# A layout of steps by a planner: small products ahead of all dense ones on TensorE

## The chip, the cores and the metric

The kernel runs on one core of a Trainium2 chip. The core has five engines with a queue each: TensorE (PE; its weight loads are listed as PEld), VectorE (DVE), ScalarE (ACT), GpSimd (POOL) and SyncE (SP, which here only issues DMAs). Each engine takes its instructions strictly in the order of its own queue, so an instruction that waits holds up all that stand behind it there. The metric is the device time of one execution in microseconds. Before the change the median of three runs is 2429.49 us (2426.96 to 2431.29).

## The reference

One decoder layer on 2048 tokens of width 1024, with 256 memory tokens. Three branches read one projection of the normed input; each branch's output is gated, projected, weighted by sigmoid gates, summed, projected once more and added to the input.

```
h = rms_norm(x, norm_g)
p = h @ w_in                      # 1024 -> 7552 columns, split into
                                  # r, k, v, decay, a, z_a | q, k, v, z_b | xq, z_c | gates
y_a = rwkv7_mix(r, k, v, decay, a, ...) * silu(z_a)      # 8 heads x 64, delta rule over time
y_b = sliding_window_sink_attn(q, k, v, ...) * silu(z_b) # 8 heads, 2 kv heads, window 128
y_c = memory_cross_attn(xq, mem, ...) * silu(z_c)        # 4 heads x 128
merged = sum_i sigmoid(gate_i) * (y_i @ w_proj_i)
out = x + merged @ w_out
```

The recurrence of branch A, per head and token, on a 64 x 64 state S:

```
sa = S @ a_t
S  = S * w_t + sa b_t^T + v_t k_t^T
y  = S @ r_t
```

## The kernel before

The 2048 tokens are worked in four superblocks of 512. Within a superblock two streams are written out and woven together by estimated durations (`weave`): `stream_r` with branch A, and `stream_f` with branches C and B, the merges of their outputs and the gates. Then follow the merge of branch A, the norm of the next superblock's input (`x_norm`) and the output projection.

**Dense and small products.** The large projections are done at about float32 accuracy as three products of fp32r halves (`gemm3`, L411 to L418: high x high, high x low, low x high). The planner calls every product whose moving operand is fp32r *dense*; its tile is 128 x 128. All others, in plain float32, are here called *small*: the transposes through TensorE (L450, L477, L724, L745, L830, L906, L1016), the column sums for norms (L466), the decay products (L637, L639), the chunk products of branch A (L694, L734, L751, L780 to L801) and the attention's products with V (L910, L1021). Many of them use only a part of the array: 64 x 64 or 32 x 32.

**Branch A's pair of heads.** `rwkv_prep` prepares a pair of heads for eight chunks of 64 tokens. VectorE builds QE, QO and BK (to L684); TensorE multiplies them in four groups of four, eight records each (L694); VectorE masks the results (L696, L697) into AB and QE, QO; ScalarE copies the diagonal blocks (L703); VectorE inverts the small triangles in 31 steps of three operations (L710 to L712); ScalarE writes the inverse into AB (L718); TensorE applies it (L734, L751), with a copy by VectorE (L735) between the two halves. V is projected, shifted (L607 to L610), transposed (L745) and copied into Z. Then `rwkv_chain` runs the chunks one after another: L787, L790 (VectorE), L795, L798 and L799 (VectorE), L801, L802 (VectorE).

**Tiles.** PSUM holds two tiles each for `mm` (projections), `rw` (branch A) and `as_` (attention), and one each for `oo` and `yps`. The tiles of one tag are opened in the order of the program, and one is free again when its last user is done.

**The planner.** The order on each engine is not the program's. `steps` reads all instructions of the program, with what each must come after, and gives each a rank: its place in the program, less 1000 for the loads and splits of weights, less 600 for what reads PSUM on other engines, and 500 more for the triangle inversion on VectorE. `lay_out` then plays the program through with a clock for each engine and estimated costs. In each turn it takes the engine that can begin soonest, lists the steps that are ready on it by then (`can`, L220) and picks one. For all engines but PE that is the step of the lowest rank. For PE it is the same, unless the tile last used was not 128 x 128: then steps of that same tile come first, and after them the lowest rank (L223, L224). A change of tile costs 95 ns in its clock, and a dense product after a small one 95 ns more. `order` puts the resulting sequences into the program, so what the planner picks is the order in which the chip's queues hold the instructions.

Of the kernel before, what the change touches and what calls it, by code (L numbers as in the profile page):

```python
# [158 lines left out]
def lay_out(tc, todo):  # L159

    metas = {tag: meta.bufs for p in tc.info.pools if p.space != bass.MemoryType.DRAM for tag, meta in p.tag_meta.items()}
    source = {t.name: t.source_name for t in tc.info.tiles}
    tags = {tag: Tag(b) for tag, b in metas.items()}
    users, opened = {}, set()
    for s in todo:
        for name in {r[0] for r in s.reads + s.writes}:
            users.setdefault(name, []).append(s)
        for r in s.writes:
            if source[r[0]] in tags and r[0] not in opened:
                opened.add(r[0])  # L170
                s.opens.append(r[0])
                tags[source[r[0]]].queue.append(r[0])
    left = {name: len(u) for name, u in users.items()}
    heads = {tag: 0 for tag in tags}
    clock = {e: 0.0 for e in NAMES.values()}
    ready, parked = {e: {} for e in clock}, set()
    orders = {e: [] for e in clock}
    missing = {s: len(s.before) for s in todo}

    def seen_by(s, b):  # L180

        if b.eng == s.eng:
            return 0 if s.eng == "PE" else b.end + 30
        return b.end + LAT[s.eng]

    def room(s):

        at = 0.0
        for name in s.opens:
            t = tags[source[name]]  # L190
            if t.queue[heads[source[name]]] != name or not t.free:
                return None
            old = t.free[0]
            if old:
                at = max([at] + [seen_by(s, b) for b in last[old].values()])
        return at

    def offer(s):
        at = room(s)
        if at is None:  # L200
            parked.add(s)
            ready[s.eng].pop(s, None)
        else:
            parked.discard(s)
            ready[s.eng][s] = max([at] + [seen_by(s, b) for b in s.before])

    last = {name: {} for name in users}
    for s in todo:
        if not missing[s]:
            offer(s)  # L210
    tile, fp32, wires = (128, 128), False, 0
    for _ in todo:
        best = None
        for e, rs in ready.items():
            if rs:
                at = max(clock[e], min(rs.values()))
                if best is None or at < best[0]:
                    best = at, e
        at, e = best
        can = [s for s, t in ready[e].items() if t <= at]  # L220
        s = min(can, key=lambda s: s.rank)
        if e == "PE":
            if tile != (128, 128) and s.tile != tile:  # L223
                s = min(can, key=lambda s: (s.tile != tile, s.rank))  # L224
            if s.tile != tile:
                at += 95
            clock[e] = at + s.busy
            if s.dense and fp32:
                clock[e] += 95
            elif s.tile != tile and s.tile[1] < 128:  # L230
                clock[e] += 49
            tile, fp32 = s.tile, not s.dense
        else:
            clock[e] = at + s.busy
        s.end = at + s.dur
        if s.bytes:
            wires = s.end = max(wires, s.end) + s.bytes / 330
        del ready[e][s]
        orders[e].append(s)
        again = set()  # L240
        for name in s.opens:
            tag = source[name]
            tags[tag].free.pop(0)
            heads[tag] += 1
            again.add(tag)
        for name in {r[0] for r in s.reads + s.writes}:
            if e not in last[name] or last[name][e].end < s.end:
                last[name][e] = s
            left[name] -= 1
            if not left[name] and source[name] in tags:  # L250
                tags[source[name]].free.append(name)
                again.add(source[name])
        for a in s.after:
            missing[a] -= 1
            if not missing[a]:
                offer(a)
        if again:
            for a in [a for rs in (parked, *ready.values()) for a in rs if any(source[n] in again for n in a.opens)]:
                offer(a)
    return orders  # L260


def order(tc, manual):

    orders = lay_out(tc, steps(list(tc.nc.cur_bb.bb.instructions), manual))
    how = mybir.DependencyInfo(mybir.DependencyClass.NoSync, mybir.DependencyReason.DATA)
    for l in orders.values():
        for a, b in zip(l, l[1:]):
            tc.add_manual_dep(b.ins, a.ins.name, how, reason="order")
# [952 lines left out]
```

## Time and profile before

| what | value |
|---|---|
| median of the runs | 2429.49 us (2426.96 to 2431.29) |
| the profiled execution | 2420.68 us, span 2418.8 us |
| mean granted TensorE clock over the span | 0.994 |
| TensorE busy | 2371.3 us, 98%, 14496 matmul records |
| VectorE busy | 1550.0 us, 64% |
| ScalarE busy | 884.2 us, 37% |
| GpSimd busy | 120.1 us, 5% |

The profile is of one execution. Times in its rows are microseconds from the start of the span. A row of the timeline has the start, the duration, the engine, the line of the kernel, the operation, the tile that is written and the tiles that are read, the part of the array for matmuls, the shapes, how many like instructions are merged, and in brackets the idle time of the engine just ahead of it with what ended it. A row of the waits has the waiting engine and line, who released it, the total in microseconds, how often and the longest. A row of the stretches has the length and then, for PE, PEld, DVE, ACT and POOL, busy microseconds and the count, then the granted clock (1.00 is full speed), the share of the DMA engines and GB/s. A plain float32 product that is no transpose stands as two records. Matmuls are pipelined, and the end of one is modelled, so that starts tell more than durations.

### The profile page before, as it was taken

Reading aid. Unit: us, or ns where it says so; the run is one execution under the profiler, and the core shown is the slowest. Engines: PE = TensorE matmul, PEld = TensorE weight load, DVE = VectorE, ACT = ScalarE, POOL = GpSimd, SP = SyncE. Lnnn points to the kernel's source line nnn. Section 1 sums busy time; section 2 is a strip of 40 time slices with the busy share of each in tenths; the row PEclk is TensorE's granted clock in tenths of the full one; section 3 lists DMA queues with packets and bytes.
Section 4 is the critical chain, followed back from the end, with each engine's and each line's share of the span. In section 5 each row is a group of like instructions: output and inputs, shape, how many; then the busy total and the mean of one; then the engine's idle time right before and its main releaser. Section 6 shows DMA issues by size and latency. Waiting matters only on the chain.

```text
span 2418.8 us, 39467 instructions
## 1 busy us (share of the span) xinstructions
PE 2371.3 (98%) x14496; PEld 1857.1 (77%) x14496; DVE 1550.0 (64%) x4926; ACT 884.2 (37%) x1961; POOL 120.1 (5%) x175
## 2 busy tenths in 40 slices
PE   7998999999999999999999999999999999999999
PEld 6777777786887777878887777777888777877887
DVE  6878778685567778852238868674143895876312
ACT  5444555434333444332113434443122344334110
POOL 1001000000000010000000001000000001000000
PEclk9998999999998999999999999999999999999999
DMA  6754555576853443446673433435566344243655
GB/s 219 253 189 149 199 195 203 201 254 216 294 180 105 150 141 105 141 141 217 200 251 111 130 116 125 139 117 204 194 209 207 103 146 136 94 140 114 209 191 191
DMA packets 142209, 416.03 MB, mean 172 GB/s; under 512 B 16193, under 2 KB 22721, under 8 KB 142017
## 3 DMA queue, kind: packets, MB, share of 16 engines
q1 hardware_dynamic: 129344, 390.44, 48.1%
q10 hardware_dynamic: 12672, 23.07, 2.8%
q8 instruction: 115, 1.88, 0.3%
q14 instruction: 78, 0.63, 0.1%
HBM read 320.66 MB, written 92.80 MB: 171 GB/s over the span
## 4 chain that ended last, share of the span: by engine, by line
PE 83%; DVE 9%; ACT 3%; DMA 3%; issue 1%; POOL 0%; SPq 0%; ACTq 0%; DVEq 0%
PE mm L416 19%; PE mm L418 19%; PE mm L417 19%; PE rw L694 2%; DMA whl<-in_w_in 2%; PE oo L1021 1%; PE mm L1067 1%; PE mm L1066 1%; PE mm L1065 1%; PE rw L801 1%; PE rw L787 1%; PE oo L910 1%; PE rw L795 1%; PE rw L734 1%; DVE whl L399 1%
## 5 line engine op out<-in xcount | busy, mean ns | idle before, releaser
L416 PE MATMUL mm<-hH,whl 128*128 128x512 f32 x1888 | 759.7, 402 | 4.8 <-ACT g L1032 3.2
L417 PE MATMUL mm<-hL,whl 128*128 128x512 f32 x1888 | 753.2, 399 | 0.0
L418 PE MATMUL mm<-hH,whl 128*128 128x512 f32 x1888 | 753.0, 399 | 0.0
L416 PEld LDWEIGHTS mm<-hH,whl 128*128 128x128 f32 x1888 | 355.4, 188 | 84.7 <-issue 7.7
L418 PEld LDWEIGHTS mm<-hH,whl 128*128 128x128 f32 x1888 | 355.2, 188 | 77.9 <-issue 3.7
L417 PEld LDWEIGHTS mm<-hL,whl 128*128 128x128 f32 x1888 | 355.5, 188 | 69.6 <-issue 1.4
L1047 DVE SCALAR_TENSOR_TENSOR g<-g,mm 128x512 f32<-128x512 f32 x64 | 43.8, 684 | 227.4 <-PE mm L418 227.4
L398 ACT ACTIVATE whl<-whl 128x512 fp32r<-128x512 f32 x174 | 109.3, 629 | 146.7 <-DMA whl<-in_w_in 72.7
L1032 ACT ACTIVATE g<-mm 128x512 f32<-128x512 f32 x96 | 57.1, 595 | 275.4 <-PE mm L418 275.0
L399 DVE TENSOR_TENSOR whl<-whl 128x512 fp32r<-128x512 f32 x174 | 119.6, 687 | 59.5 <-ACT whl L398 57.2
L417 PE MATMUL mm<-yl,whl 128*128 128x512 f32 x384 | 151.0, 393 | 0.0
L416 PE MATMUL mm<-yh,whl 128*128 128x512 f32 x384 | 150.8, 393 | 0.0
L418 PE MATMUL mm<-yh,whl 128*128 128x512 f32 x384 | 150.6, 392 | 0.0
L711 DVE TENSOR_TENSOR ibc<-ibc,Yi 128x248 f32<-128x248 f32 (+30 forms) x496 | 143.9, 290 | 10.1
L710 DVE STREAM_SHUFFLE ibc<-Nc 128x248 f32<-128x248 f32 (+30 forms) x496 | 148.8, 312 | 0.0
L793 ACT ACTIVATE SP<-Z,Pl 64x64 f32<-64x64 f32 x256 | 88.4, 345 | 155.1 <-DVE Z L802 151.5
L712 DVE TENSOR_TENSOR Yi<-Yi,ibc 128x248 f32<-128x248 f32 (+30 forms) x496 | 141.0, 284 | 2.0
L1001 ACT ACTIVATE g<-g,mxs,st 128x256 f32<-128x256 f32 (+1 forms) x128 | 74.4, 585 | 74.8 <-DVE mxs L994 74.8
L802 DVE SCALAR_TENSOR_TENSOR Z<-rw,Pl,SP 64x64 f32<-64x64 f32 x224 | 63.5, 283 | 44.9 <-PE rw L801 41.7
L416 PEld LDWEIGHTS mm<-yh,whl 128*128 128x128 f32 x384 | 72.1, 188 | 15.3 <-DVE g L1047 0.2
L417 PEld LDWEIGHTS mm<-yl,whl 128*128 128x128 f32 x384 | 72.1, 188 | 15.0
L418 PEld LDWEIGHTS mm<-yh,whl 128*128 128x128 f32 x384 | 72.1, 188 | 14.9
(1769 smaller groups left out, 3760.7 us busy)
## 6 DMA issues: line engine op xcount, KB each, us to landing
whl<-k SPq DMA_DIRECT2D x474, 512.0 KB, 3.3
k<-whl SPq DMA_DIRECT2D x158, 512.0 KB, 3.3
whl<-in_w_in SPq DMA_DIRECT2D x118, 256.0 KB, 3.2
g<-in_x ACTq DMA_DIRECT2D x32, 256.0 KB, 5.6
out<-g ACTq DMA_DIRECT2D x32, 256.0 KB, 4.9
whl<-in_w_proj SPq DMA_DIRECT2D x24, 256.0 KB, 2.9
rt<-in_x ACTq DMA_DIRECT2D x24, 256.0 KB, 5.2
km<-mk SPq DMA_DIRECT2D x16, 256.0 KB, 2.7
```

The costliest lines, as they stand in the source:

```text
L398: S.activation(w[:, 0], raw, AF.Copy)
L399: V.tensor_tensor(w[:, 1], raw, w[:, 0].bitcast(F32), op=ALU.subtract)
L416: PE.matmul(out, lh, rh, start=i == 0, stop=False)
L417: PE.matmul(out, lh, rl, start=False, stop=False)
L418: PE.matmul(out, ll, rh, start=False, stop=i == n - 1)
L710: V.stream_shuffle(bc[:, :, :n], Nc[:, :, s + 1:], [s] * 32)
L711: V.tensor_tensor(bc[:, :, :n], bc[:, :, :n], Y[:, :, s:s + 1].to_broadcast([128, NC_, n]), op=ALU.mult)
L712: V.tensor_tensor(Y[:, :, s + 1:], Y[:, :, s + 1:], bc[:, :, :n], op=ALU.add)
L793: S.activation(SP[h, i], Z[h, i, e, c], AF.Copy, scale=g[4][h, c:c + 1])
L802: upds = [V.scalar_tensor_tensor(Sst[h, g[0]] if c == NC_ - 1 else Z[h, i, e, c + 1], pS[h, i], g[4][h, c:c + 1], SP[h, i], op0=ALU.mult, ...
L1001: S.activation(prs[b][:, i, m0:], prs[b][:, i, m0:], AF.Exp, scale=r2[:, b, i:i + 1], bias=mx[:, b, i:i + 1], accum_out=mx[:, b, 2 + i:3 + i])
L1032: S.activation(t, gp, AF.Tanh, scale=0.5)
```

## The change

In `lay_out`, the choice on PE. Before, the lowest rank was taken, or after a tile other than 128 x 128 the same tile first. Now dense steps come after all others that are ready; among the others, those of the tile last used come first if the last product was a small one; within that the lowest rank decides. Nothing else in the planner, in its costs or in the program is different.

```diff
@@ -220,8 +220,7 @@
         can = [s for s, t in ready[e].items() if t <= at]
         s = min(can, key=lambda s: s.rank)
         if e == "PE":
-            if tile != (128, 128) and s.tile != tile:
-                s = min(can, key=lambda s: (s.tile != tile, s.rank))
+            s = min(can, key=lambda s: (s.dense, fp32 and s.tile != tile, s.rank))
             if s.tile != tile:
                 at += 95
             clock[e] = at + s.busy
```

`fp32` is true if the product picked last on PE was a small one. Since the planner's clocks go on from each choice, the sequences of the other engines are drawn anew as well.

## The prediction

> **What bounds the kernel now.** I read the page's busy times first, then PE's own waits, then the timeline round its longest repeated wait, and last the clock by stretches. The page:
>
> ```profile
> span 2418.8 us, 39467 instructions
> PE 2371.3 (98%) x14496; PEld 1857.1 (77%) x14496; DVE 1550.0 (64%) x4926; ACT 884.2 (37%) x1961; POOL 120.1 (5%) x175
> ```
>
> TensorE is busy for 98% of the span. No product is removed or added by the change, so only three things can move the time: PE's idle time (2418.8 - 2371.3 = 47.5 us), the price of switching between dense and small products, and the granted clock. PE's own waits, longest first:
>
> ```profile
> PE rw L450 <- DVE g L445: 10.0, 2, 9.5
> PE rw L734 <- ACT AB L718: 5.6, 3, 1.9
> PE rw L694 <- DVE QE L684: 3.5, 4, 2.6
> ```
>
> The first is the start of the kernel: nothing is there to do before the first loads and the norm, and the change can't touch it. The second is three equal stalls of 1.86 us, one in each of the later three superblocks, ahead of L734 (the products with the inverse of the small triangle). Here they are, two of them with the dense product behind the small stretch that follows:
>
> ```profile
> 739.07 0.66 PE L734 MATMUL rw<-ibc,AB 32*32 32x32 f32 x16 [1.86 <-ACT AB L718]
> 753.44 0.40 PE L416 MATMUL mm<-hH,whl 128*128 128x512 f32 x1
> ...
> 1327.17 0.66 PE L734 MATMUL rw<-ibc,AB 32*32 32x32 f32 x16 [1.86 <-ACT AB L718]
> 1336.34 0.40 PE L416 MATMUL mm<-hH,whl 128*128 128x512 f32 x1
> ...
> 1910.46 0.66 PE L734 MATMUL rw<-ibc,AB 32*32 32x32 f32 x16 [1.85 <-ACT AB L718]
> ```
>
> The reader should see that the projections (L416 to L418) are used up by then, and that the next one into a new `mm` tile comes only after the small products: 9.17 us after L734 in the second superblock drawn here (1336.34 - 1327.17), 14.37 us in the first (753.44 - 739.07). The same work took 5.2 us longer the first time, and the clock says why:
>
> ```profile
> core 0: us, PE busy (x) PEld busy (x) DVE busy (x) ACT busy (x) POOL busy (x), PEclk, DMA share, GB/s
> 694.90:700.00 5.10, 5.10 (x25) 3.95 (x23) 0.56 (x1) 0.00 (x0) 0.10 (x1) 1.00 0.09 26
> 700.00:739.00 39.00, 37.16 (x205) 30.30 (x204) 36.04 (x154) 12.01 (x27) 1.61 (x5) 1.00 0.35 109
> 739.70:753.40 13.70, 13.70 (x83) 9.34 (x83) 3.53 (x9) 5.54 (x16) 1.26 (x2) 0.50 0.03 9
> 1327.20:1340.90 13.70, 13.35 (x119) 10.18 (x120) 5.74 (x13) 9.04 (x25) 1.26 (x2) 1.00 0.16 50
> 1910.40:1924.10 13.70, 13.30 (x118) 10.19 (x119) 5.75 (x13) 9.02 (x26) 1.26 (x2) 1.00 0.11 33
> ```
>
> After the first stall PE ran at half clock for 13.7 us; after the two others at full clock.
>
> **The change, part by part.** *Small ahead of dense.* What a small product gains is the time it now lies ready behind dense ones of lower rank. The stall shows the case that matters. VectorE writes QE and QO, which L694 multiplies:
>
> ```profile
> 694.05 0.69 DVE L684 TENSOR_TENSOR QO<-rr__7309,Pt 64x512 f32<-64x512 f32 x1
> 694.77 0.69 DVE L685 TENSOR_TENSOR rr__7309<-rr__7309,rk__7144 128x512 f32<-128x512 f32 x1
> 700.71 0.69 DVE L848 SCALAR_TENSOR_TENSOR g<-g,mm 128x512 f32<-128x512 f32 x1 [5.25 <-ACT g L847]
> 701.31 0.68 DVE L696 TENSOR_TENSOR AB<-rw,gmask 64x512 f32<-64x512 f32 x1
> ...
> 708.45 0.44 DVE L710 STREAM_SHUFFLE ibc<-Nc 128x248 f32<-128x248 f32 x1
> ...
> 737.28 0.17 DVE L712 TENSOR_TENSOR Yi<-Yi,ibc 128x8 f32<-128x8 f32 x1
> ```
>
> ```profile
> 693.36 1.89 PE L910 MATMUL oo<-g,vm 128*128 128x256 f32 x8
> 694.90 0.58 PE L416 MATMUL mm<-hH,whl 128*128 128x512 f32 x1
> ...
> 699.65 0.39 PE L418 MATMUL mm<-hH,whl 128*128 128x512 f32 x1
> 699.97 0.37 PE L694 MATMUL rw<-QE,BK 64*128 64x128 f32 x1
> ...
> 700.86 0.27 PE L694 MATMUL rw<-QO,BK 64*128 64x128 f32 x1
> 701.07 0.50 PE L416 MATMUL mm<-hH,whl 128*128 128x512 f32 x1
> 701.40 0.39 PE L417 MATMUL mm<-hL,whl 128*128 128x512 f32 x1
> ```
>
> QO is done at 694.74 (694.05 + 0.69). L694 starts at 699.97, 5.2 us later, behind 21 dense products from 694.90 on, and VectorE meanwhile idles 5.25 us. Then it is full: 36.04 of the 39 us from 700 to 739, with the inversion (L710 to L712) from 708.45 to 737.45, whose end PE waits for. With the new choice L694 follows L910 at about 694.9, so the masks (L696, L697) fill VectorE's idle 5.25 us and the inversion can end up to that much earlier, of which PE needs 1.86. The dense products moved back are then still there for PE's gaps around L734. The other two superblocks have the same pattern:
>
> ```profile
> 1282.19 0.69 DVE L684 TENSOR_TENSOR QO<-rr__12827,Pt 64x512 f32<-64x512 f32 x1
> 1288.85 0.69 DVE L848 SCALAR_TENSOR_TENSOR g<-g,mm 128x512 f32<-128x512 f32 x1 [5.25 <-ACT g L847]
> ...
> 1865.51 0.69 DVE L684 TENSOR_TENSOR QO<-rr__18345,Pt 64x512 f32<-64x512 f32 x1
> 1872.17 0.69 DVE L848 SCALAR_TENSOR_TENSOR g<-g,mm 128x512 f32<-128x512 f32 x1 [5.25 <-ACT g L847]
> ```
>
> Bounds of this term: nothing, if the inversion is held by something else, and all three stalls, 3 x 1.86 = 5.6 us. I take -5.6, since 5.25 us of room against 1.86 is ample. What is late next are the hops of the same chain through L735, L745 and L751; the dense products kept back cover them.
>
> *The clock after the stall.* The half clock cost 5.2 us (14.37 - 9.17) behind one stall of three. Bounds: 0 (it comes anyway) and -5.2. I take -5.2: with the idle time gone, nothing in these rows is left that would start the drop.
>
> The Trainium skill (TensorE: Matmul & The Clock Gate, Part 1) says that the clock is gated by activity over free-running windows of about 3.4 us, so that the drop depends on where in a window the idle time falls. That agrees with one drop after three equal stalls; by it the unprofiled runs may hold more or fewer such drops than this profile, which only widens the range.
>
> *More and smaller pieces.* A group taken as soon as it is ready may come in more pieces than a group taken when its rank comes up. The price of a cut:
>
> ```profile
> 968.23 0.40 PE L418 MATMUL mm<-hH,whl 128*128 128x512 f32 x1
> 968.46 0.40 PE L416 MATMUL mm<-hH,whl 128*128 128x512 f32 x1
> 968.70 0.27 PE L477 MATMUL rw<-c_ident,rep 128*128 128x128 f32 x1
> 968.73 0.49 PE L417 MATMUL mm<-hL,whl 128*128 128x512 f32 x1
> 969.05 0.27 PE L477 MATMUL rw<-c_ident,rep 128*128 128x128 f32 x1
> 969.08 0.48 PE L418 MATMUL mm<-hH,whl 128*128 128x512 f32 x1
> ```
>
> Dense starts lie 0.23 apart, and 0.35 with one transpose between (969.08 - 968.73): at least 0.12 with the transpose itself. Round L694 it is 0.09 going in (699.97 - 699.65 - 0.23), 0.10 from the last small start (701.07 - 700.86 - 0.11) and 0.10 at the next dense one (701.40 - 701.07 - 0.23), 0.29 in all. I take 0.2 a cut. How many come or go, the trace doesn't say. L694 above joins the L910 in front of it, which saves one. The rwkv_prep of each of 16 head pairs has four such groups that may split once (+16), and the 16 pairs of branch B, with transposes and products (L1016, L1021) in pieces, may have two more cuts each (+32). Joins like that one there may be one for each of the 12 head pairs of the later superblocks. Bounds: -12 joins and +48 cuts, -2.4 to +9.6 us. I take +10 cuts, +2.0, near the lower end: groups like L734 and L477 in the rows above already follow another engine step by step and go when they are ready, whatever the rule.
>
> *Small ones of the last tile first.* Before, this held after every tile but 128x128; now after every small product. It reorders neighbours inside a run of small products; a switch there costs no more than a cut, either way, at a few places: 0, inside the bounds of the cuts.
>
> *What else moves.* The statistics (L466), the transposes of BK (L724) and of x for the next superblock (L450) and the decay products (L637, L639) also go earlier where they wait behind dense ones. They take their PSUM tiles sooner, but each tag is opened in program order, so that nothing else could have used them. I cost them at nothing: what hides them is the dense supply, and without it they would be on PE's path as they are now. Their readers on ScalarE, VectorE and POOL come earlier, too, and POOL has room (5% busy). No DMA is added; SP's queue with the weights is laid out by the same clock and shifts with it.
>
> *Sum.* Against the profiled execution, 2420.7 us with 2418.8 of span: -5.6 - 5.2 + 2.0 = -8.8, so 2411.9. The median of the runs, 2429.5, lies 8.8 above that execution; the same difference off it gives 2420.7. I round to 2421.
>
> **The rivals.** *A: nothing comes of it.* The whole order is drawn anew, the inversion starts earlier but gets a later place among VectorE's other work (it is the lowest in rank there), and the stall stays. For it: VectorE is 92% busy from 700 to 739 (36.04 of 39). Against: the idle 5.25 us lies ahead of just that stretch. Only the cuts remain: 2429.5 + 2.0 = 2431.5.
>
> *B: the pieces, slower.* If every group splits as above, 48 cuts at 0.2 are 9.6 us; with the clock drop staying they outweigh the stalls from 28 cuts on (5.6 / 0.2). If the stalls stay too, it is 2429.5 + 9.6 = 2439. For it: VectorE releases its transposes' inputs one by one, as L477 shows. Against: the groups of the chain, the most numerous, are already taken when ready.
>
> *C: the clock, slower.* Small products run together leave stretches without dense ones, and each superblock gets a half clock. The stalls go, one drop stays, two come: 2429.5 - 5.6 + 2.0 + 2 x 5.2 = 2436. Against: 1327.20 to 1340.90 was such a stretch, at 1.00.
>
> The Trainium skill (same page, Part 4) says that transposes don't count as activity for the clock as other products do, which speaks for C; no run here shows that yet.
>
> **How the numbers follow.** Forecast 0.58, A 0.17, B 0.18, C 0.07. Differences under 0.2% (4.9 us) can't be told from none. Faster: the forecast with its own range, from 2406 (all three stalls gone, a further two drops of 5.2 gone in runs that have them, joins of 2.4: 2429.5 - 5.6 - 15.6 - 2.4 = 2405.9) to 2424.6: 0.60, with a little of B. Within: A and small sums, 0.14. Slower: B, C and part of A, 0.26. The range that leaves two in ten out reaches from 2405 to 2437.
>
> **What would show it.** Right: L694 starts within 0.5 us of its QO in the first pair of each later superblock; VectorE's wait of 5.25 before L848 is gone; PE's wait for AB L718 falls from 5.6 us to under 1; no half clock near 740; PE's busy time grows by no more than 2 us. Wrong: the wait for L718 is still there; new waits of PE on VectorE of over 1 us (L694, L450, L1021), with dense products queued behind; a half clock in more stretches; PE's busy time up by 5 us or more, which would be the pieces.

## The result and the profile after

The changed kernel takes 2435.81 us (median of ten, 2431.45 to 2441.48) against 2428.68 us for the kernel before (ten runs, 2423.96 to 2433.67): a ratio of 1.0031, with a 95% interval of 1.002 to 1.0042. It is slower by 7 us; 2421 had been forecast, and a gain. The profiled execution took 2435.84 us, with a span of 2434.0. Line numbers after L222 are one lower than before the change.

The page's first lines and PE's waits, after:

```profile
span 2434.0 us, 39511 instructions
PE 2392.6 (98%) x14496; PEld 1875.2 (77%) x14496; DVE 1550.2 (64%) x4926; ACT 886.2 (36%) x1961; POOL 126.3 (5%) x175
```

```profile
PE rw L449 <- DVE g L444: 10.5, 2, 9.9
PE rw L636 <- ACT Z L746: 2.2, 6, 0.5
PE rw L476 <- DVE rep L475: 2.0, 2, 1.0
PE rw L723 <- DVE QE L696: 1.9, 1, 1.9
```

The wait for AB (L718, now L717), 5.6 us before, is gone from the list. Yet PE is busy for 21.3 us more (2392.6 - 2371.3) with the same 14496 records. So the change did remove the stalls, and the products themselves take longer.

To see which, I added up, over both traces, the time from the start of each matmul record to the start of the next, under the line of the first; idle time is taken out, and half of what ran at half clock (a granted clock of 0.50):

| us, first profile of before against after | before | after | difference |
|---|---|---|---|
| transposes of BK (L724, now L723) | 10.3 | 18.5 | +8.2 |
| decay products (L637 and L639) | 19.9 | 25.6 | +5.7 |
| products of QE and QO (L694) | 55.0 | 60.0 | +5.1 |
| dense products (with the scores) | 1914.3 | 1914.4 | +0.1 |
| all other small products | 356.1 | 358.4 | +2.3 |
| sum | 2355.6 | 2376.9 | +21.3 |
| idle, first to last matmul | 33.8 | 27.6 | -6.2 |
| lost to the half clock | 15.4 | 15.4 | 0 |

Three kinds of products make 18.9 of the 21.3 us. All three read one half of the partitions, and each has a partner that reads the other half. In the list of groups their busy time (which counts overlapping records once) shows it for the transposes, first before, then after:

```profile
L724 PE MATMUL rw<-c_ident,BK 64*128 64x64 f32 x160 | 8.6, 238 | 0.0
L724 PE MATMUL rw<-c_ident,whl 64*128 64x64 f32 x96 | 4.3, 229 | 0.0
```

```profile
L723 PE MATMUL rw<-c_ident,BK 64*128 64x64 f32 x160 | 14.5, 242 | 1.9 <-DVE QE L696 1.9
L723 PE MATMUL rw<-c_ident,whl 64*128 64x64 f32 x96 | 7.4, 230 | 0.0
```

256 transposes before and after, each as long as ever (238 and 229, 242 and 230 ns), but 12.9 us of TensorE before and 21.9 after. The timeline says why. Before, the sixteen of a head pair, upper and lower half in turn:

```profile
725.40 0.71 PE L724 MATMUL rw<-c_ident,BK 64*128 64x64 f32 x16
726.04 0.50 PE L416 MATMUL mm<-hH,whl 128*128 128x512 f32 x1
```

After, eight of one half and then, four dense products later, eight of the other; and the decay products of another head pair, each alone:

```profile
710.29 0.71 PE L723 MATMUL rw<-c_ident,BK 64*128 64x64 f32 x8
710.93 0.50 PE L415 MATMUL mm<-hH,whl 128*128 128x512 f32 x1
...
712.06 0.71 PE L723 MATMUL rw<-c_ident,BK 64*128 64x64 f32 x8
...
870.87 1.12 PE L636 MATMUL rw<-lwla,rep 64*128 64x512 f32 x2
871.93 0.50 PE L415 MATMUL mm<-yh,whl 128*128 128x512 f32 x1
...
873.17 1.12 PE L638 MATMUL rw<-lwla,rep 64*128 64x512 f32 x2
```

Eight records take the 0.71 us that sixteen took. The groups of L694 were already apart in part in the kernel before: a single one, eight records, stands here, against sixteen in 1.10 us (699.97 to 701.07) in the prediction's rows:

```profile
703.46 1.13 PE L694 MATMUL rw<-QE,BK 64*128 64x128 f32 x8
704.51 0.50 PE L416 MATMUL mm<-hH,whl 128*128 128x512 f32 x1
```

Next to each other, two halves run at the same time: before, L637 and L639 of a head pair start together,

```profile
675.03 0.69 PE L637 MATMUL rw<-lwla,rep 64*128 64x512 f32 x1
675.03 0.69 PE L639 MATMUL rw<-lwla,rep 64*128 64x512 f32 x1
675.56 0.59 PE L637 MATMUL rw<-lwla,rep 64*128 64x512 f32 x1
675.57 0.59 PE L639 MATMUL rw<-lwla,rep 64*128 64x512 f32 x1
676.09 0.50 PE L416 MATMUL mm<-hH,whl 128*128 128x512 f32 x1
```

and the four records are over in 1.06 us (676.09 - 675.03), while after, L636 alone takes 1.06 (871.93 - 870.87). The Trainium skill (TensorE: Matmul & The Clock Gate, Part 3) says that products on different row groups of the array run concurrently, with starts a few ns apart; the trace agrees, with starts 0.00 to 0.01 us apart.

Why the change parts them: each half writes a PSUM tile of its own, and the two tiles come free, or the two inputs get ready, at different times. The old rule let both wait behind dense products until their rank came up, by when both were mostly ready. The new rule takes the first half as soon as its own tile and inputs are there, all eight of it, and the other half later. The planner doesn't see the price: `cost_PE` charges a product the same with its partner beside it or alone.

### The profile page after: what moved, and what is told of

It reads as the page before. It is cut to its first block, busy times and chain, and to the rows that moved or that the text cites. A ratio compares the mean times of both kernels' runs of the same rounds, so it can differ in the third digit from the quotient of the medians.

```text
span 2434.0 us, 39511 instructions
## 1 busy us (share of the span) xinstructions
PE 2392.6 (98%) x14496; PEld 1875.2 (77%) x14496; DVE 1550.2 (64%) x4926; ACT 886.2 (36%) x1961; POOL 126.3 (5%) x175
## 4 chain that ended last, share of the span: by engine, by line
PE 83%; DVE 7%; ACT 4%; DMA 3%; issue 1%; POOL 1%; SPq 0%; ACTq 0%; POOLq 0%; DVEq 0%
PE mm L415 19%; PE mm L417 19%; PE mm L416 19%; PE rw L693 2%; PE oo L1020 1%; PE mm L1064 1%; PE mm L1065 1%; PE mm L1066 1%; PE rw L786 1%; PE rw L800 1%; PE rw L794 1%; PE oo L909 1%; DMA whl<-in_w_in 1%; PE rw L723 1%; DMA rt<-in_x 1%
## 5 line engine op out<-in xcount | busy, mean ns | idle before, releaser
L416 PE MATMUL mm<-hL,whl 128*128 128x512 f32 x1888 | 752.5, 399 | 0.0
L416 PEld LDWEIGHTS mm<-hL,whl 128*128 128x128 f32 x1888 | 357.0, 189 | 73.5 <-issue 6.1
L415 PE MATMUL mm<-yh,whl 128*128 128x512 f32 x384 | 153.6, 400 | 0.0
L416 PE MATMUL mm<-yl,whl 128*128 128x512 f32 x384 | 153.2, 399 | 0.0
L417 PE MATMUL mm<-yh,whl 128*128 128x512 f32 x384 | 152.8, 398 | 0.0
L416 PEld LDWEIGHTS mm<-yl,whl 128*128 128x128 f32 x384 | 72.2, 188 | 14.5 <-issue 0.2
```

Source lines behind the costliest of these rows:

```text
L415: PE.matmul(out, lh, rh, start=i == 0, stop=False)
L416: PE.matmul(out, lh, rl, start=False, stop=False)
L417: PE.matmul(out, ll, rh, start=False, stop=i == n - 1)
```

## The experiments

**Tying the pairs.** Undo only the parting, keep the change. In `steps`, the members of a pair of halves get the union of what each of them must come after, and the first of them opens both PSUM tiles:

```diff
+    for names in tied:
+        ss = [byname[n] for n in names]
+        need = set().union(*(s.before for s in ss)) - set(ss)
+        for s in ss:
+            new = (need | ({ss[0]} if s is not ss[0] else set())) - s.before
+            for b in new:
+                b.after.append(s)
+            s.before |= new
+        ss[0].also = [n for n in dict.fromkeys(r[0] for s in ss for r in s.writes)]
...
-        for c in range(NC_):
-            for pk, h in zip(pks, (EV, OD)):
-                PE.transpose(pk[:, c], BK[h, c], ident[h, h])
+        tied.append([PE.transpose(pk[:, c], BK[h, c], ident[h, h]).ins.name
+                     for c in range(NC_) for pk, h in zip(pks, (EV, OD))])
```

First for the transposes of BK and the decay products alone:

> The changed kernel, with one thing added to the planner: the 16 transposes of BK of a head pair (two PSUM tiles, the upper and the lower half of the partitions in turn) and the two decay products of a head pair become ready together, when both their tiles are free and all their inputs are there, so that upper and lower half stand next to each other in PE's queue again. The products of QE and QO stay as the change has them. Theory (the changed rule takes the half whose tile is free first and so parts pairs that ran side by side; in the trace of the changed kernel the time up to the next start grew by 8.2 us after the transposes of BK and by 6.0 us after the decay products): 2435.8 - 14.2 = about 2421.6, faster than before. Rival (the whole order drawn anew is worse, the parted pairs are only one face of it): within 4 us of 2436.

Measured: 2421.94 us, ratio to the kernel before 0.9973 (0.9957 to 0.9988). The transposes in the list of groups of its profile, where they have line L733:

```profile
L733 PE MATMUL rw<-c_ident,BK 64*128 64x64 f32 x160 | 8.0, 240 | 1.5 <-DVE QO L708 1.5
L733 PE MATMUL rw<-c_ident,whl 64*128 64x64 f32 x96 | 4.3, 229 | 0.0
```

The transposes are back at 12.3 us, and the kernel takes what was expected to within a microsecond. That it came so near is in part luck: in the sums of this profile the two kinds take 15.3 us less than in the changed kernel (14.2 had been counted, with 6.0 for the decay products where the table above has 5.7), the half clock 3.5 us less (11.9), and the dense products, for a reason that stays open, 5.1 us more. With these pairs kept, the changed rule is faster than the old one, so undoing the parting takes back more than the whole loss of 7 us.

Then with the products of QE and QO tied as well:

> As the run before, with the four groups of products of QE and QO tied as well (each two groups of one half of the chunks become ready together). Theory: a tied group of 16 records took 1.10 us to the next dense start (699.97 to 701.07), two single ones of 8 took 1.05 and 1.09; about 24 of the 32 pairs of groups are apart in the changed kernel, so 24 x 1.04 = 25 us more than the run before gains: about 2397. Rival (holding QE back until QO is there delays the inversion on VectorE, and the stalls ahead of L734 come back): 2397 + 5.6 or more, up to no gain over the run before.

Measured: 2416.27 us, ratio 0.9959 (0.9944 to 0.9973): 6 us better than the run before, not 25. By the sum of times to the next start, L694 did lose 23.7 us (61.4 to 37.7). But it has to wait now, for VectorE and for both tiles, in a stretch where VectorE is late. PE's waits (L703 is L694 here), and the stretch round the longest of them:

```profile
PE rw L460 <- DVE g L455: 10.7, 2, 10.1
PE rw L703 <- DVE QE L695: 5.8, 1, 5.8
PE mm L426 <- ACT g L1041: 4.3, 3, 1.5
PE rw L703 <- DVE QO L707: 2.7, 4, 1.6
```

```profile
208.00:225.00 17.00, 12.59 (x59) 9.91 (x61) 15.67 (x33) 3.42 (x8) 2.83 (x3) 0.52 0.19 63
```

The 5.8 us stand in the first superblock, and PE runs at about half clock behind them. Idle time rose from 27.3 to 41.3 us against the run before, and the loss to the half clock from 11.9 to 22.2: 24.3 us given back in the profiles of a 31 us gain in the sum (2367.4 to 2336.3). The first theory's size was wrong because it left out what holding back a half costs. The rival's stalls ahead of L734 did not come back: what PE still waits for AB is 0.3 us.

**The pairs tied under the old rule.**

> The kernel before with its old rule, and all three kinds of pairs tied as in the second run. In the kernel before the transposes were together nearly always, the products of QE and QO in fewer than half of the cases. Theory: 18 pairs of groups x 1.04 = 19 us less, 2428.7 - 19 = about 2410, slower than the second run by what the changed rule is worth once the pairs are kept (the 5.6 us of stalls and some cuts, 6 to 13 us). Rival (the changed rule is worth nothing even so): equal to the second run within 3 us.

Measured: 2432.23 us, ratio 1.0015 (1.000 to 1.003). Both expectations miss. L694 fell as under the new rule (55.0 to 38.6 us), but dense products run out again while the chain is on its way, now ahead of the column sums, and each of three such stalls is followed by half clock, of which one stretch is shown behind the waits; PE's waits in this profile (L477 is the column sums, L466 before; L427 and L704 are L416 and L694; two more tiles of L477 wait 2.0 us each, as the last row does):

```profile
PE rw L461 <- DVE g L456: 10.2, 2, 9.6
PE mm L427 <- ACT g L1042: 9.3, 8, 3.6
PE rw L704 <- DVE BK L691: 4.3, 1, 4.3
PE rw L488 <- DVE rep L487: 2.7, 4, 1.9
PE as__13408 L477 <- ACT g L880: 2.0, 1, 2.0
```

```profile
1329.60:1343.20 13.60, 13.60 (x94) 9.82 (x93) 4.64 (x12) 6.46 (x18) 1.26 (x2) 0.50 0.07 18
```

Idle time is 46.2 us and the loss to the half clock 37.5. So with all pairs tied the changed rule is worth 16 us (2432.2 - 2416.3), more than its stalls. The granted clocks of the runs say where: their medians, 0.9845 here and 0.991 there, make 38 and 22 us lost (an estimate: one less the clock, times the span), a difference of the same 16 us.

**The price of parting, by itself.** The kernel before, with two loops exchanged:

```diff
-        for c in range(NC_):
-            for pk, h in zip(pks, (EV, OD)):
+        for pk, h in zip(pks, (EV, OD)):
+            for c in range(NC_):
                 PE.transpose(pk[:, c], BK[h, c], ident[h, h])
```

> The kernel before, with the two loops round the transposes of BK exchanged in the program: eight of the upper half first, then eight of the lower half. No product, tile or wait is added or gone, and the planner's rule is the old one. Theory (parting the halves costs by itself): 0.5 us for each of 16 head pairs, since eight starts in one half take the 0.49 us that sixteen in turn took: 8 us more, 2428.7 + 8 = 2436.7. Rival (the two halves do not overlap; what the changed kernel lost there is switches to and from dense products): no difference, within 3 us of 2428.7.

Measured: 2433.72 us, ratio 1.0027 (1.0011 to 1.0043), 5.3 us slower, more than the rival's 3 us and less than the theory's 8. The sixteen transposes still stand in one run, only not in turn:

```profile
724.63 1.01 PE L724 MATMUL rw<-c_ident,BK 64*128 64x64 f32 x16
725.58 0.50 PE L416 MATMUL mm<-hH,whl 128*128 128x512 f32 x1
```

0.95 us to the next dense start against 0.64 (726.04 - 725.40): 0.31 a head pair, not 0.5, and 14.9 us in all against 10.3. The rest of the 0.5 in the changed kernel is the cut: there a second run of small products starts for each pair that dense products part, and two runs of eight at 0.64 take 1.28, which is 0.33 more than 0.95. The halves do overlap, and losing that costs time with no switch more.

**The two halves of the change.** Dense products last, but the old rule for tiles:

```diff
-            s = min(can, key=lambda s: (s.dense, fp32 and s.tile != tile, s.rank))
+            s = min(can, key=lambda s: (s.dense, tile != (128, 128) and s.tile != tile, s.rank))
```

> The first half of the change alone: dense steps come after all others that are ready; among the others the old rule holds (the tile last used first, unless it was 128x128). Theory (the parted pairs come from taking what is ready ahead of dense steps, not from the order among small ones): as the changed kernel, 2435.8 within 4 us, with the time after the transposes of BK and after the decay products as long as there. Rival (preferring the last tile parts them, since it keeps on with one half): both short again, about 2422.

Measured: 2436.43 us, ratio 1.0033 (1.002 to 1.0047), the time of the changed kernel. The times to the next start after the transposes (18.6 us) and the decay products (25.6) are those of the changed kernel too. The new rule for tiles in place of the old one does nothing that can be measured; the whole effect is in putting small products first.

**Half-array products by rank.** The change for all small products but L637, L639, L694 and L724:

```diff
-            s = min(can, key=lambda s: (s.dense, fp32 and s.tile != tile, s.rank))
+            s = min(can, key=lambda s: (s.dense or s.tile == (64, 128), fp32 and s.tile != tile, s.rank))
```

> The change for all small products but those that read one half of the partitions into all of the output (L637, L639, L694, L724): those take their turn by rank among the dense ones, as before. Theory: the pairs are mostly together again (14 to 20 us less than the changed kernel), but L694 waits behind dense products again, so that the three stalls ahead of L734 are back (5.6 us and the clock behind them, 5 us each): 2420 to 2430. Rival (the stalls went because of the other small products that go first): no wait of PE for L718, 2415 or less.

Measured: 2449.83 us, ratio 1.0093 (1.0072 to 1.0114), outside what either expected. The transposes are together again (10.3 us), and the stalls are back (L733 is the product with AB here):

```profile
PE rw L449 <- DVE g L444: 10.3, 2, 9.9
PE rw L733 <- ACT AB L717: 6.0, 3, 2.2
PE mm L415 <- ACT g L1031: 4.1, 3, 1.4
PE rw L693 <- DVE QE L696: 3.7, 5, 0.9
```

So it is L694 (or another of these four lines) going first that removed the wait for AB; the other small products going first did not. (This run puts the four lines behind all other small products, too, which is later than in the kernel before, so it is not that kernel's order for them.) Against the first profile of the kernel before, the span is 24.2 us longer (2443.0 - 2418.8): the products take 8.9 us more by the sum of times to the next start, in 638 runs of small products against 604, idle time is 6.7 us more (40.5) and the loss to the half clock 8.5 us more (23.9).

**The kernel before, profiled again.**

> The kernel before once more, for a second profile of it. Theory (the half clock after the stalls ahead of L734 comes by chance, and the first profile, 8 us under the median of the runs, held fewer of them than most): half clock after two or three of the three stalls, and a span above 2418.8 us by about 5 us for each one more. Rival (the first profile is typical, and the profiled execution is faster for another reason): half clock near 740 alone and a span within 2 us of 2418.8.

Measured: 2425.72 us in one run, a span of 2423.9. The three stretches behind the stalls, in this profile and in that of the exchanged loops:

```profile
738.90:752.50 13.60, 13.22 (x95) 9.08 (x95) 3.77 (x10) 5.88 (x16) 1.26 (x2) 0.54 0.08 32
1326.70:1340.30 13.60, 12.83 (x116) 9.77 (x117) 6.02 (x14) 8.91 (x24) 1.27 (x2) 1.00 0.16 53
1909.70:1923.30 13.60, 13.02 (x95) 9.27 (x95) 3.97 (x11) 6.06 (x17) 1.27 (x2) 0.54 0.10 37
```

```profile
739.10:752.70 13.60, 13.60 (x89) 9.39 (x86) 3.56 (x10) 5.77 (x17) 1.26 (x2) 0.52 0.03 12
1329.60:1339.80 10.20, 10.20 (x67) 7.37 (x64) 2.65 (x8) 4.96 (x14) 1.26 (x2) 0.53 0.00 0
1916.70:1926.90 10.20, 10.20 (x71) 7.37 (x68) 2.80 (x8) 4.67 (x14) 1.26 (x2) 0.53 0.01 2
```

The same three stalls were followed by a half clock once in the first profile, twice here and three times with the loops exchanged, and with one more drop here the span was 5.1 us longer (2423.9 - 2418.8). The first profile had been a fortunate one. The granted clocks of the other runs, which are on record, say by how much: the median is 0.989 over 35 runs of the kernel before, about 27 us lost (an estimate, as above), where the first profile at 0.994 lost 15.4; over the ten runs of the changed kernel it is 0.9935, about 16 us. That is why the two profiled executions differ by 15 us and the medians by only 7: typical runs of the kernel before lose some 11 us more to the clock than that profile did, and the changed kernel has no such stalls.

**A version that beats both.** All pairs tied, but those of QE and QO only from the second superblock on:

```diff
+            if sb:
+                tied.append(both)
```

> The changed kernel with all three kinds of pairs tied, but the products of QE and QO only from the second superblock on. In the run with all of them tied, PE waited 5.8 us for QE near 205 us and ran at half clock for 17 us behind it, both in the first superblock, where VectorE is late. Theory (tying costs only where VectorE is late): the 5.8 us and some of the clock come back, 2416.3 - 6 to 10 = about 2408, better than both kernels. Rival (the waits move to the later superblocks as well, or the first superblock's stay): 2414 to 2418.

Measured: 2415.05 us, ratio 0.9948 (0.9935 to 0.9961). Not told apart from tying all of them (0.9959, 0.9944 to 0.9973), and not the 2408 of the theory: the wait of 5.8 us is gone, but L694 takes 7.0 us more (44.7 against 37.7), all of it in the first superblock, where its pairs are parted. The time lies in the rival's range, but not for the rival's reason. Both are some 13 us faster than the kernel before and 20 faster than the changed one.

## Why the prediction was wrong

**What bounds the kernel:** right. PE stays at 98%, and all that was won or lost is in its idle time, its products or its clock.

**The stalls ahead of L734, -5.6 us:** right in size, in the line that caused it and in the mechanism, but not in how far L694 could move. L694 of the first pair in the second superblock did not start at 694.9. Its input came 9 us later than before; for 8 of them the whole kernel was late by then (2250 dense products had started by 689.2 before and by 697.3 after):

```profile
703.01 0.69 DVE L683 TENSOR_TENSOR QO<-rr__7309,Pt 64x512 f32<-64x512 f32 x1
```

```profile
703.28 0.71 PE L693 MATMUL rw<-QE,BK 64*128 64x128 f32 x4
703.84 0.34 PE L693 MATMUL rw<-QO,BK 64*128 64x128 f32 x1
...
743.47 0.39 PE L415 MATMUL mm<-hH,whl 128*128 128x512 f32 x1
743.78 0.69 PE L733 MATMUL rw<-ibc,AB 32*32 32x32 f32 x16
```

QO ended at 703.70, and its products began at 703.84, with no dense one ahead, as the rule says. Between L694's four groups there was then one dense product instead of thirteen. Counted over both traces, 2304 dense products had started before the inversion began and 2278 after the change. So 26 moved behind its start, as the prediction had it: 11 from ahead of the first group, where it had expected 21, 12 from between the groups and 3 from behind the last. PE uses 15 of them by L733 (127 dense products from the start of the inversion on, 112 before), 3.5 us at 0.23, and comes to it with no idle time. That L694 or another of the four lines must go first for it, the run with half-array products by rank shows.

**The clock after the stall, -5.2 us:** the drop near 740 is gone, but the profile after has drops elsewhere, three of them in the first superblock and one of 3.4 us from 1347.3, and the sum is the same 15.4 us. The argument that nothing was left to start a drop looked only at the stretch behind that stall. Stretches of that profile:

```profile
142.40:149.20 6.80, 6.80 (x32) 5.11 (x33) 2.98 (x9) 1.91 (x7) 0.00 (x0) 0.50 0.33 111
214.20:224.30 10.10, 8.24 (x39) 7.10 (x38) 8.56 (x18) 7.00 (x13) 2.83 (x3) 0.50 0.24 85
350.60:357.40 6.80, 6.80 (x24) 5.20 (x24) 6.16 (x17) 2.19 (x6) 0.00 (x0) 0.50 0.40 129
739.70:753.40 13.70, 13.45 (x109) 9.31 (x108) 6.13 (x32) 7.14 (x19) 0.00 (x0) 1.00 0.32 108
```

In typical runs of the kernel before, the clock cost some 11 us more than in the profile, as the second profile's section says, and the changed kernel doesn't lose that, so that here the prediction erred to the careful side. The 8.8 us that it carried over from the profiled execution to the median, as if they stayed, were lost clock of this kind, by these estimates.

**More and smaller pieces, +2.0 us:** this is the step that failed, together with the nothing that was put on what else moves (below). It took ten more cuts at 0.2 us. Counted over the two traces, runs of small products between dense ones number 604 before and 604 after: no cuts were added on balance. What was missing in the term is that a group of one half costs about as much as both halves in turn. The step even priced L694's four groups that may split once at a cut each (+16, 3.2 us), while a tied pair of groups takes 1.10 us to the next dense start (701.07 - 699.97) and a single group 1.05 (704.51 - 703.46 in the same profile). The rows that it quoted held the mechanism: the L694 records at 699.97 and 700.86 were two of sixteen that start in pairs. L694 measured +5.1 us. With the two kinds that were put at nothing, the three kinds of pairs measured +18.9 us, against a bound of +9.6 for all pieces together; 18.9 in place of 2.0 turns the -8.8 of the sum into +8.1, a loss.

**Small ones of the last tile first, 0:** right, by the run with the old rule for tiles (2436.43 against 2435.81).

**What else moves, at nothing:** wrong for the transposes of BK (+8.2 us) and the decay products (+5.7), which go earlier in halves, and so the larger part of the 18.9 us. That "each tag is opened in program order, so that nothing else could have used them" was true, and beside the point: the second tile of a pair can come free later than the first, and the products of the first then go alone.

**The rivals:** A did not come, since the wait for AB is gone. B named the right side and the right term, and an increase of PE's busy time of 5 us or more as its sign, which came (21.3); but its mechanism, cuts one by one, is not what happened (604 runs before and after). C did not come: no stretch of small products in the later superblocks dropped for more than 3.4 us.

## What to carry to other kernels

Where an order of products is chosen by a planner, products that use different halves of the array are one unit: look in the timeline for records that start at the same time, and tie them or price them, before changing what goes first. A rule that takes the first ready thing is right about latency and parts whatever becomes ready in two steps. A profile's count of cuts or switches says nothing of overlap; the time to the next start, summed by line, does. And before a profile is taken as the base of a sum, its granted clock should be compared with that of the other runs: here 0.994 against a median of 0.989 were some 11 us.

## What the runs showed of the hardware

Sixteen transposes of 64 x 64 on alternate halves of the partitions took TensorE 0.64 us to the next dense start; in one run but half by half 0.95; eight of one half alone 0.64 (710.93 - 710.29). Order inside a queue is enough to lose the overlap.

A stall of 1.86 us ahead of a stretch of small products was followed by a half clock of 10 to 14 us in six of nine cases, over three executions with the same stalls. The Trainium skill (TensorE: Matmul & The Clock Gate, the section Why this matters for your kernels) asks for no gaps over about 3 us between bursts; here the half clock followed shorter ones, and the traces decide. Whether the stall or the small products behind it start the drop, the runs do not separate: the changed kernel, with full clock there (739.70 to 753.40), has no stall and has 31 dense products of the projections in that stretch, where the kernel before has none.
